# A two-layer hybrid trunk on one core: products put in order of length, the first output projection in wider blocks, and background steps called more often

## The chip, the core and the metric

The kernel runs on one core of a Trainium2 chip. The metric is the device time of one execution in microseconds (us); the profile is of one execution, taken apart from the timed runs. TensorE (PE) multiplies, VectorE (DVE) and ScalarE (ACT) do elementwise work, GpSimd (POOL) small work and some transfers, and SyncE (SP) issues the weight transfers. A difference of under 0.2% is about what a measurement of this kernel can't tell from none.

## The reference, cut to what matters

256 tokens of 2048 features pass through two layers. Layer 0 is a gated delta net, layer 1 an attention over chunks; each has one input projection of 2048 to 8192 features (q, k, v and the gate z), a mixer over 16 heads of 128, and an output projection of 2048 to 2048, whose result is added to the input.

```
def gated_deltanet(h, w_in, conv_w, a_log, dt_bias, out_norm_w, w_out):
    proj = h @ w_in
    qkv = silu(causal_depthwise_conv(proj[..., :3 * A_INNER], conv_w))
    z = proj[..., 3 * A_INNER:4 * A_INNER]
    ...                      # q, k normed; beta, g per head from 32 more columns
    decay = exp(where(tri_incl, gc[..., :, None] - gc[..., None, :], -inf))
    sol = triangular_solve(eye + lower, rhs)          # per chunk of 64
    ...                      # scan over the chunks gives o
    o = rms_norm(o, out_norm_w) * silu(z)
    return o.reshape(bsz, t, A_INNER) @ w_out

def chunk_band_attention(h, w_in, q_norm_w, k_norm_w, rel_bias, w_out):
    ...                      # softmax over a band of keys, times silu(z)
    return o @ w_out

for i in range(DEPTH):
    h = h + mixer[i](rms_norm(h, norm_w[i]))
```

## The kernel before

All matrices are f32. A product of f32 matrices is made of three products of rounded parts: the weights are split into `whi` and `wlo`, the activations into a high and a low part (`xb[:, kt, 0]` and `xb[:, kt, 1]`), and high x high, high x low and low x high are summed in PSUM. The features of a 2048-wide operand lie in 16 slices of 128, which the text calls kt 0 to 15.

**The weights** come in 320 chunks of 512 KB, in the order of the list `plan`. `chunk` uses one and first calls `fetch` until the chunk three further on is asked for: a transfer into `wt` (SP), a cast to `whi` on ACT (L191) and a subtraction to `wlo` on DVE (L192). There are three buffers of `whi` and of `wlo`, so a chunk's cast waits until TensorE has finished with the chunk three before it.

**The kinds of block.** `half` makes 256 output features: a chunk is four kt of 256 columns, and for each kt and each of two slices of 128 features (s) there are two products with the weights as the stationary operand, one of 512 moving columns (`whi` on both parts of the activations, L232) and one of 256 (`wlo` on the high part, L233). The text calls these two a pair; a half block is 32 pairs. `features` makes 512 output features out of three products of 256 columns for each kt and s (L224, L226, L227), a triple; a block is 64 triples in eight chunks of two kt. `tokens` makes 512 features with the activations as the stationary operand, in products of 512 columns (L239 to L241). A block accumulates in a tile `psp` of PSUM, of which there are two; `joined` moves a half block out (ACT copies the second product's part into `ev`, DVE adds the rest, L288 and L289), and `ev` has two buffers too. Small products, such as the transposes, use `pss`.

**The background.** Everything that isn't a projection is written as generators in two lanes, `bgq` and `bg2`. After each kt (each second kt in a half block) `chunk` calls `step(rate)`, which advances `rate` times one generator to its next `yield`, the lanes in turn; `drain` runs all of them to their end. So the place of a small product in TensorE's order, and of a vector operation in DVE's, follows from these calls, and from a scheduler in the framework which sorts the instructions of each engine by a timeline of its own.

**Order of the work.** Layer 0: q (a block in 512 features, then six half blocks), k (eight half blocks), three token blocks of z, v (eight half blocks), the last token block of z, then the first output projection. `decays` makes the decay factors, `q_conv` and `k_small` convolve, `inversion` solves the triangular systems, `v_small`, `v_back` and `gated` make a group of four heads of the mixer's output and split it into `gmem` (tile `g`); group gi gives kt 4gi to 4gi+3 of the output projection, and `ready` holds a product back until its kt is done.

**The first output projection before** (kernel end of `tile_hybrid_trunk`): eight half blocks. The first two are cut: kt 0 to 11 of both, then `drain`, then kt 12 to 15 of both, since the last head group comes last. `ha_small` takes a finished block, adds x (fetched by POOL's queue into tile `dl`, which the mixer has used until then) and splits the sum for layer 1.

Of the kernel before, what the change touches and what calls it, by code (L numbers as in the profile page):

```python
# [7 lines left out]
F32 = mybir.dt.float32  # L8
# [3 lines left out]
ALU = mybir.AluOpType  # L12
AX = mybir.AxisListType

P = 128
D = 2048
T = 256
H = 16
KT = D // P
# [4 lines left out]
NWARM = 12  # L24
TIE0 = 4
TIE = 2


C_CONV = 0
# [10 lines left out]
def tile_hybrid_trunk(  # L40
# [11 lines left out]
    nc = tc.nc  # L52
# [24 lines left out]
    xv = xT.rearrange("(k p) t -> p k t", p=P)  # L77
# [51 lines left out]
    def wide(w, col, c0=0, c1=CPB):  # L129
        return [(w, col, c, 512) for c in range(c0, c1)]  # L130
# [4 lines left out]
    def halves(w, col, n):  # L135
        return [x for j in range(n) for x in half(w, col + 256 * j)]
# [9 lines left out]
    def cut_halves(w, col):  # L146

        p = []
        for c0, c1 in ((0, CUTH), (CUTH, CPH)):
            for j in range(2):  # L150
                p += half(w, col + 256 * j, c0, c1)
        return p + halves(w, col + 512, 6)

    plan += cut_halves(a_w_out, 0)
    plan += cut_halves(b_w_in, 6144)
    for gi in range(4):
        plan += wide(b_w_in, 4096 + 512 * gi)
# [48 lines left out]
    def step(n=1):  # L206

        while now:
            now.pop(0)()
        for _ in range(n):  # L210
            lanes = (bgq, bg2) if turn[0] else (bg2, bgq)
            turn[0] ^= 1
            for lane in lanes:
                if advance(lane):
                    break
# [10 lines left out]
        pe.matmul(ps, lhsT=hi[:, j, fs], rhs=xb[:, kt, 1, :], start=False, stop=False, skip_group_check=True)  # L226
        pe.matmul(ps, lhsT=lo[:, j, fs], rhs=xb[:, kt, 0, :], start=False, stop=(kt == KT - 1), skip_group_check=True)  # L227

    def features2(ps, s, j, kt, hi, lo, xb):

        fs = slice(s * P, (s + 1) * P)
        pe.matmul(ps, lhsT=hi[:, j, fs], rhs=xb[:, kt, :, :], start=(kt == 0), stop=False, skip_group_check=True)  # L232
        pe.matmul(ps[:, 0, :], lhsT=lo[:, j, fs], rhs=xb[:, kt, 0, :], start=False, stop=(kt == KT - 1),  # L233
                  skip_group_check=True)

    def tokens(ps, t, j, kt, hi, lo, xb):
        ts_ = slice(t * P, (t + 1) * P)
# [2 lines left out]
        pe.matmul(ps, lhsT=xh, rhs=lo[:, j, :], start=False, stop=False)  # L240
        pe.matmul(ps, lhsT=xl, rhs=hi[:, j, :], start=False, stop=(kt == KT - 1))  # L241

    KINDS = {"features": (features, 4), "half": (features2, 2), "tokens": (tokens, 2)}

    def chunk(kind, ps, xb, rate=1, pre=None):
        i = state["use"]
        state["use"] += 1
        while state["next"] < min(i + 1 + LOOK, len(plan)):
            fetch()
        hi, lo = fetched.pop(i)  # L250
        kc = KC * 512 // plan[i][3]
        ks = [plan[i][2] * kc + j for j in range(kc)]
        f, ns = KINDS[kind]
        if i == len(plan) - 1:

            out_pre(ps)
            for s in range(ns):
                fs = slice(s * P, (s + 1) * P)
                for j, kt in enumerate(ks):
                    for w, a in ((hi, 0), (hi, 1), (lo, 0)):  # L260
                        pe.matmul(ps[:, s, 0, :], lhsT=w[:, j, fs], rhs=xb[:, kt, a, :], start=False,
                                  stop=(kt == KT - 1 and w is lo), skip_group_check=True)
                out_part(s, ps)
            return
        for j, kt in enumerate(ks):
            if pre is not None:
                pre(kt)
            for s in range(ns):
                f(ps[:, s], s, j, kt, hi, lo, xb)
            if kind != "half" or j % 2:  # L270
                step(rate)

    def acc(kind):

        shape = {"features": [P, 4, T], "half": [P, 2, 2, T], "tokens": [P, 2, 512]}[kind]
        return psp.tile(shape, F32, name="psp", tag="psp")

    def block(kind, xb, rate=1, pre=None):
        ps = acc(kind)
        for _ in range(CPH if kind == "half" else CPB):  # L280
            chunk(kind, ps, xb, rate, pre)
        return ps
# [423 lines left out]
    def ready(mem):  # L706

        def pre(kt):
            while mem["done"] <= kt:
                step()  # L710
        return pre
# [97 lines left out]
        split(x_sb[:, kt, :], kt, 0, xb)  # L809

    for gi in range(4):
        ps = pair(xb) if gi else block("features", xb, pre=x_split)
        if gi == 0:
            bgq.append(x_stats())
        bgq.append(q_conv(gi, ps))
        if gi == 0:
            bgq.append(decays())
        else:
            if gi == 1:
                bgq.append(q_rest(0))  # L820
            bgq.append(q_rest(gi))
    for gi in range(4):
        bgq.append(k_small(gi, pair(xb)))
    for gi in range(3):
        ps = block("tokens", xb)
        if gi == 0:
            drain()
        bgq.append(za_small(gi, ps))
        if gi == 0:
            bgq.append(inversion())  # L830
# [7 lines left out]

    hmem = {}

    def ha_small(n, ps):
        if n == 0:
            m = slot("dl", 48)
            hmem["m"] = m
            hmem["h"] = m[:, :2 * D].rearrange("p (k t) -> p k t", k=KT)
            hmem["x"] = split_tiles()
            hmem["s"] = m[:, 8192:9216].rearrange("p (j t) -> p j t", j=4)
            hmem["done"] = 0
        xb, h = hmem["x"], hmem["h"][:, 2 * n:2 * n + 2, :]
        j = n // 2  # L850
        if n % 2 == 0:
            ks = slice(4 * j, 4 * j + 4)
            nc.gpsimd.dma_start(out=hmem["h"][:, ks, :], in_=xv[:, ks, :])
        ev = work.tile([P, 2, T], F32, name="ev", tag="ev")
        act.copy(out=ev, in_=ps[:, :, 1, :])  # L855
        yield 1
        if n in (0, 2):

            dve.tensor_copy(out=hmem["h"][0:1, 4 * j + 8, 0:1], in_=ev[0:1, 0, 0:1])
        dve.tensor_tensor(out=h, in0=ps[:, :, 0, :], in1=h, op=ALU.add)  # L860
        dve.tensor_tensor(out=h, in0=h, in1=ev, op=ALU.add)
        yield 1
        for i in range(2):
            split(h[:, i, :], 2 * n + i, 1, xb)
            hmem["done"] = 2 * n + i + 1
            yield 1
        if n % 2:
            squares4(hmem["h"][:, 4 * j:4 * j + 4, :], hmem["s"][:, j, :])
            yield 1

# [14 lines left out]
                    z=slot("tt", 16).rearrange("p (h t) -> p h t", h=H))  # L885
        yield 1

    def a_done(j, ps):
        bgq.append(ha_small(j, ps))

    pa = [acc("half") for _ in range(2)]
    for n in (CUTH, CPH - CUTH):
        for j in range(2):
            if n != CUTH and j == 0:
                drain()
            for _ in range(n):
                chunk("half", pa[j], gmem["b"], 3, ready(gmem))
            if n != CUTH:
                a_done(j, pa[j])
    for j in range(2, 8):  # L900
        a_done(j, block("half", gmem["b"], 2))


    bgq.append(b_setup())
# [231 lines left out]
```

## Time and profile before

| | |
|---|---|
| three timed runs | 1033.37, 1034.61, 1035.04 us (median 1034.61) |
| profiled execution: its time, its span | 1032.16 us, 1030.5 us |
| TensorE busy | 1009.8 us (98% of the span) |
| VectorE busy | 698.7 us (68%) |
| ScalarE busy | 525.4 us (51%) |
| granted TensorE clock, mean | 0.993 of full |

The profiled execution is 1.7 us longer than its span (launch and end), and 2.45 us shorter than the median of the runs. Ends of matmuls are modelled and overlap, so "busy" on TensorE is no measure of speed; the spacing of starts is.

### The profile page before, as it was taken

What the parts mean: (1) busy time and instruction counts of PE and PEld (TensorE: products, weight loads), DVE (VectorE), ACT (ScalarE), POOL (GpSimd) and SP (SyncE); (2) the same over time, 40 slices, a digit from 0 to 9 for tenths busy, and PEclk for the clock granted to TensorE, in tenths of its full rate; (3) what the DMA queues carried; (4) which work ended last, traced back from release to release, by engine and by line L of the source; (5) the groups of instructions that cost most, each with busy time, mean ns of one, the idle gap of its engine ahead of it and who ended that gap; (6) DMA issues with size and microseconds to landing.
All of it is one profiled execution on the core that took longest, in us unless ns stands there. A gap on an engine that the chain in (4) does not pass through costs nothing.

```text
span 1030.5 us, 15332 instructions
## 1 busy us (share of the span) xinstructions
PE 1009.8 (98%) x5966; PEld 874.0 (85%) x5966; DVE 698.7 (68%) x1117; ACT 525.4 (51%) x726; POOL 74.4 (7%) x91
## 2 busy tenths in 40 slices
PE   8999999999999999987999999999999999999998
PEld 7988888887888989886888888888888888889986
DVE  7789899997997688655666555444456666666553
ACT  8465765455445555443554444444445545555442
POOL 1004000212000000001000000000011010101000
PEclk9999999999999999998999999999999999999999
DMA  9654565554773454543656776666665555554562
GB/s 309 177 164 132 157 182 164 147 162 141 209 197 107 123 160 132 161 162 123 207 188 181 221 217 213 188 200 188 198 186 169 158 166 161 163 162 147 177 221 72
DMA packets 137832, 177.54 MB, mean 172 GB/s; under 512 B 7584, under 2 KB 97824, under 8 KB 137760
## 3 DMA queue, kind: packets, MB, share of 16 engines
q1 hardware_dynamic: 136608, 172.38, 56.3%
q0 software_dynamic: 1152, 4.19, 1.1%
q8 instruction: 46, 0.75, 0.3%
q14 instruction: 26, 0.21, 0.1%
HBM read 174.46 MB, written 2.10 MB: 171 GB/s over the span
## 4 chain that ended last, share of the span: by engine, by line
PE 93%; DVE 3%; ACT 1%; issue 1%; DMA 0%; SPq 0%; POOL 0%; DVEq 0%; ACTq 0%; POOLq 0%
PE psp L232 29%; PE psp L233 15%; PE psp L240 11%; PE psp L239 11%; PE psp L241 11%; PE psp L227 2%; PE psp L226 2%; PE psp L224 2%; PE pss L540 2%; DVE wlo L192 1%; PE pss L737 1%; PE pss L972 1%; PE pss L991 1%; PE pss L1027 1%; ACT whi L191 1%
## 5 line engine op out<-in xcount | busy, mean ns | idle before, releaser
L192 DVE TENSOR_TENSOR wlo<-wt,whi 128x1024 fp32r<-128x1024 f32 (+1 forms) x321 | 392.8, 1226 | 254.1 <-ACT whi L191 250.7
L191 ACT CAST whi<-wt 128x1024 fp32r<-128x1024 f32 (+1 forms) x321 | 336.3, 1049 | 403.8 <-PE psp L232 187.8
L232 PE MATMUL psp<-xb,whi 128*128 128x512 f32 x960 | 341.0, 398 | 2.1 <-DVE ev L289 2.0
L233 PE MATMUL psp<-xb,wlo 128*128 128x256 f32 x960 | 270.3, 282 | 0.0
L232 PEld LDWEIGHTS psp<-xb,whi 128*128 128x128 f32 x960 | 180.8, 189 | 43.8 <-DVE ev L289 2.7
L241 PE MATMUL psp<-whi,xb 128*128 128x512 f32 x512 | 201.2, 393 | 0.0
L240 PE MATMUL psp<-wlo,xb 128*128 128x512 f32 x512 | 200.9, 392 | 0.3 <-DVE wlo L192 0.3
L239 PE MATMUL psp<-whi,xb 128*128 128x512 f32 x512 | 199.8, 390 | 0.0
L233 PEld LDWEIGHTS psp<-xb,wlo 128*128 128x128 f32 x960 | 181.9, 189 | 1.5 <-DVE wlo L192 0.5
L232 PE MATMUL psp<-g,whi 128*128 128x512 f32 x376 | 135.9, 405 | 2.6 <-ACT ev L855 1.6
L240 PEld LDWEIGHTS psp<-wlo,xb 128*128 128x128 f32 x512 | 96.1, 188 | 20.7 <-DVE wlo L192 1.2
L239 PEld LDWEIGHTS psp<-whi,xb 128*128 128x128 f32 x512 | 96.2, 188 | 19.7
L241 PEld LDWEIGHTS psp<-whi,xb 128*128 128x128 f32 x512 | 96.2, 188 | 19.4
L233 PE MATMUL psp<-g,wlo 128*128 128x256 f32 x376 | 106.5, 284 | 0.0
L232 PEld LDWEIGHTS psp<-g,whi 128*128 128x128 f32 x376 | 71.8, 191 | 20.8 <-ACT ev L855 1.9
L233 PEld LDWEIGHTS psp<-g,wlo 128*128 128x128 f32 x376 | 72.3, 192 | 0.2
L483 DVE SCALAR_TENSOR_TENSOR cv<-raw,sm,cv 128x255 f32<-128x255 f32 (+2 forms) x144 | 62.0, 479 | 1.7 <-ACT cv L481 1.5
L224 PE MATMUL psp<-g,whi 128*128 128x256 f32 x128 | 36.8, 288 | 0.0
L226 PE MATMUL psp<-g,whi 128*128 128x256 f32 x128 | 36.7, 287 | 0.0
L227 PE MATMUL psp<-g,wlo 128*128 128x256 f32 x128 | 36.3, 284 | 0.0
L955 POOL TENSOR_SCALAR ssn<-ssn,uh 128x4 f32<-128x4 f32 x16 | 8.3, 530 | 271.9 <-DVE ssn L953 271.9
L481 ACT ACTIVATE cv<-raw,sm 128x256 f32<-128x256 f32 x48 | 21.4, 500 | 7.7 <-DVE raw L304 4.8
(240 smaller groups left out, 988.2 us busy)
## 6 DMA issues: line engine op xcount, KB each, us to landing
wt<-in_b_w_in_dram SPq DMA_DIRECT2D x128, 512.0 KB, 3.7
wt<-in_a_w_in_dram SPq DMA_DIRECT2D x127, 512.0 KB, 4.0
wt<-in_a_w_out_dram SPq DMA_DIRECT2D x32, 512.0 KB, 3.4
wt<-in_b_w_out_dram SPq DMA_DIRECT2D x32, 512.0 KB, 3.8
g<-in_xT_dram SPq DMA_DIRECT2D x8, 256.0 KB, 4.5
dl<-in_xT_dram POOLq DMA_DIRECT2D x4, 512.0 KB, 5.5
dl<-in_relb_dram POOLq DMA_DIRECT2D x4, 512.0 KB, 5.1
out_dram<-cv SPq DMA_DIRECT2D x2, 512.0 KB, 3.6
```

The lines of the kernel that those rows point to most:

```text
L191: act.copy(out=hi[:, js], in_=wt[:, js])
L192: dve.tensor_tensor(out=lo[:, js], in0=wt[:, js], in1=hi[:, js].bitcast(F32), op=ALU.subtract)
L224: pe.matmul(ps, lhsT=hi[:, j, fs], rhs=xb[:, kt, 0, :], start=(kt == 0 and s % 2 == 0), stop=False, skip_group_check=True)
L226: pe.matmul(ps, lhsT=hi[:, j, fs], rhs=xb[:, kt, 1, :], start=False, stop=False, skip_group_check=True)
L227: pe.matmul(ps, lhsT=lo[:, j, fs], rhs=xb[:, kt, 0, :], start=False, stop=(kt == KT - 1), skip_group_check=True)
L232: pe.matmul(ps, lhsT=hi[:, j, fs], rhs=xb[:, kt, :, :], start=(kt == 0), stop=False, skip_group_check=True)
L233: pe.matmul(ps[:, 0, :], lhsT=lo[:, j, fs], rhs=xb[:, kt, 0, :], start=False, stop=(kt == KT - 1), skip_group_check=True)
L239: pe.matmul(ps, lhsT=xh, rhs=hi[:, j, :], start=(kt == 0), stop=False)
L240: pe.matmul(ps, lhsT=xh, rhs=lo[:, j, :], start=False, stop=False)
L241: pe.matmul(ps, lhsT=xl, rhs=hi[:, j, :], start=False, stop=(kt == KT - 1))
L481: act.activation(out=cv[:, i, :], in_=raw[:, i, :], func=AF.Copy, scale=conv_w(i0 + i, 3))
L483: dve.scalar_tensor_tensor(out=cv[:, i, s:], in0=raw[:, i, :T - s], scalar=conv_w(i0 + i, 3 - s), in1=cv[:, i, s:], op0=ALU.mult, op1=ALU.add)
```

## The change

Three edits. In half blocks the products of two kt (GROUP) are issued by length: the four of 512 columns, then the four of 256. The first two blocks of the first output projection (eight half blocks before) become blocks of 512 features of the kind `features`, cut at the same kt 12; four half blocks follow. And `decays` goes into the second lane, the pairs of q call `step(2)`, the second and third token block of z too; the cut blocks call `step(2)` after each kt, where they called `step(3)` after each second one.

```
@@ -151,7 +152,10 @@
-    plan += cut_halves(a_w_out, 0)
+    for c0, c1 in ((0, CUT), (CUT, CPB)):
+        for j in range(2):
+            plan += wide(a_w_out, 512 * j, c0, c1)
+    plan += halves(a_w_out, 1024, 4)
@@ -226,12 +230,16 @@
-    def features2(ps, s, j, kt, hi, lo, xb):
-        fs = slice(s * P, (s + 1) * P)
-        pe.matmul(ps, lhsT=hi[:, j, fs], rhs=xb[:, kt, :, :], start=(kt == 0), stop=False, skip_group_check=True)
-        pe.matmul(ps[:, 0, :], lhsT=lo[:, j, fs], rhs=xb[:, kt, 0, :], start=False, stop=(kt == KT - 1),
-                  skip_group_check=True)
+    def features2(ps, hi, lo, js, ks, xb):
+        both = [(s, j) for j in js for s in range(2)]
+        for s, j in both:
+            pe.matmul(ps[:, s], lhsT=hi[:, j, s * P:(s + 1) * P], rhs=xb[:, ks[j], :, :], start=(ks[j] == 0), stop=False,
+                      skip_group_check=True)
+        for s, j in both:
+            pe.matmul(ps[:, s, 0, :], lhsT=lo[:, j, s * P:(s + 1) * P], rhs=xb[:, ks[j], 0, :], start=False,
+                      stop=(ks[j] == KT - 1), skip_group_check=True)
@@ -262,13 +270,21 @@
+        if kind == "half":
+            for j in range(0, kc, GROUP):
+                js = range(j, j + GROUP)
+                if pre is not None:
+                    for jj in js:
+                        pre(ks[jj])
+                features2(ps, hi, lo, js, ks, xb)
+                step(rate)
+            return
@@ -809,12 +825,12 @@
-        ps = pair(xb) if gi else block("features", xb, pre=x_split)
+        ps = pair(xb, 2) if gi else block("features", xb, pre=x_split)
...
-            bgq.append(decays())
+            bg2.append(decays())
...
-        ps = block("tokens", xb)
+        ps = block("tokens", xb, 2 if gi else 1)
@@ -846,25 +863,28 @@
+        two = len(ps.shape) == 4
+        if two:
+            ev = work.tile([P, 2, T], F32, name="ev", tag="ev")
+            act.copy(out=ev, in_=ps[:, :, 1, :])
...
+        dve.tensor_tensor(out=h, in0=ps[:, :, 0, :] if two else ps, in1=h, op=ALU.add)
+        if two:
+            dve.tensor_tensor(out=h, in0=h, in1=ev, op=ALU.add)
@@ -885,20 +905,20 @@
-    pa = [acc("half") for _ in range(2)]
-    for n in (CUTH, CPH - CUTH):
+    pa = [acc("features") for _ in range(2)]
+    for n in (CUT, CPB - CUT):
         for j in range(2):
-            if n != CUTH and j == 0:
+            if n != CUT and j == 0:
                 drain()
             for _ in range(n):
-                chunk("half", pa[j], gmem["b"], 3, ready(gmem))
-            if n != CUTH:
-                a_done(j, pa[j])
-    for j in range(2, 8):
-        a_done(j, block("half", gmem["b"], 2))
+                chunk("features", pa[j], gmem["b"], 2, ready(gmem))
+            if n != CUT:
+                a_done(j, pa[j], 4 * j, 4 * j + 4)
+    for j in range(4):
+        a_done(j + 2, block("half", gmem["b"], 2), 8 + 2 * j, 10 + 2 * j)
```

The order of the built programs shows where this moves instructions. First TensorE at the cut of the first output projection, before: L760 to L762 are the last products of the mixer (`v_back`, last group), L798 the transposes of `gated` for that group, L232 and L233 the output projection.

```order
L760 MATMUL pss<-dl 128x128
L761 MATMUL pss<-dl 128x128
L762 MATMUL pss<-dl 128x128
L798 MATMUL pss<-ident,dl 128x128 x8
L232 MATMUL psp<-g,whi 128x512
L233 MATMUL psp<-g,wlo 128x256
L232 MATMUL psp<-g,whi 128x512
```

The same place after (the lines of the mixer are 16 higher, the products of the output projection are L228, L230 and L231). Between the two pieces stand 76 products of the output projection, counted without the rows shown of the second piece's transposes; 175 stand ahead of the first piece.

```order
L776 MATMUL pss<-dl 128x128
L777 MATMUL pss<-dl 128x128
L778 MATMUL pss<-dl 128x128
L230 MATMUL psp<-g,whi 128x256
L231 MATMUL psp<-g,wlo 128x256
...
L230 MATMUL psp<-g,whi 128x256
L814 MATMUL pss<-ident,dl 128x128 x2
L231 MATMUL psp<-g,wlo 128x256
L228 MATMUL psp<-g,whi 128x256
L230 MATMUL psp<-g,whi 128x256
L231 MATMUL psp<-g,wlo 128x256
L814 MATMUL pss<-ident,dl 128x128 x6
```

Where nothing stood between the mixer's last product and the transposes, 76 products stand there now; after the transposes 33 more come before the first one that needs kt 12 (288 products of the two cut blocks don't need it: 12 kt, 4 slices, 3 products, 2 blocks).

Second, ScalarE early in the k stage, before: L509 are squares of `q_rest`, L191 the weight cast, L288 the copy that moves a half block out of `psp`, L481 the first taps of a convolution.

```order
L191 CAST whi<-wt 128x1024 x2
L509 ACTIVATE raw<-pss 128x512 x2
L191 CAST whi<-wt 128x1024
L288 COPY ev<-psp 128x512
L481 ACTIVATE cv<-raw,sm 128x256 x4
L191 CAST whi<-wt 128x1024
L288 COPY ev<-psp 128x512
```

And after (L525, L195, L304 and L497 are the same lines there):

```order
L195 CAST whi<-wt 128x1024
L525 ACTIVATE raw<-pss 128x512 x2
L195 CAST whi<-wt 128x1024 x2
L497 ACTIVATE cv<-raw,sm 128x256 x2
L304 COPY ev<-psp 128x512
L497 ACTIVATE cv<-raw,sm 128x256 x2
L195 CAST whi<-wt 128x1024
L304 COPY ev<-psp 128x512
```

The copy out of `psp` has moved behind two taps of the convolution, and a weight cast ahead of it; the rest of the stage's order is nearly as it was.

Third, TensorE in any half block, before:

```order
L232 MATMUL psp<-xb,whi 128x512
L233 MATMUL psp<-xb,wlo 128x256
L232 MATMUL psp<-xb,whi 128x512
L233 MATMUL psp<-xb,wlo 128x256
```

and after:

```order
L238 MATMUL psp<-xb,whi 128x512 x4
L241 MATMUL psp<-xb,wlo 128x256 x4
```

The same products stand in runs of four of one length.

## Rows read from the trace of the kernel before

**Rows 1.** The page: busy us (share of the span) xinstructions of each engine, and the chain that ended last, by engine.

```profile
PE 1009.8 (98%) x5966; PEld 874.0 (85%) x5966; DVE 698.7 (68%) x1117; ACT 525.4 (51%) x726; POOL 74.4 (7%) x91
...
PE 93%; DVE 3%; ACT 1%; issue 1%; DMA 0%; SPq 0%; POOL 0%; DVEq 0%; ACTq 0%; POOLq 0%
```

**Rows 2.** Busy time of the stretch around the cut of the first output projection: us from and to, their length, then busy us of PE, PEld, DVE, ACT and POOL with the number of instructions, the granted TensorE clock (1.00 is full), the DMA share and GB/s.

```profile
461.00:481.00 20.00, 11.47 (x46) 9.28 (x46) 8.32 (x13) 4.89 (x7) 4.17 (x4) 0.74 0.26 85
```

**Rows 3.** TensorE in order of time at the cut of the first output projection: start us, us, then the instruction; in brackets the idle time before it and who ended it.

```profile
460.64 0.39 PE L762 MATMUL pss<-dl 128*128 128x128 f32 x2
466.99 2.15 PE L798 MATMUL pss<-ident,dl 128*128 128x128 f32 x8 [5.97 <-DVE dl L694]
470.06 0.80 PE L232 MATMUL psp<-g,whi 128*128 128x512 f32 x1 [0.92 <-DVE g L803]
...
470.86 0.63 PE L232 MATMUL psp<-g,whi 128*128 128x512 f32 x1
...
475.35 0.54 PE L232 MATMUL psp<-g,whi 128*128 128x512 f32 x1
...
478.16 0.28 PE L233 MATMUL psp<-g,wlo 128*128 128x256 f32 x1
480.07 0.47 PE L232 MATMUL psp<-g,whi 128*128 128x512 f32 x1 [1.64 <-ACT ev L855]
```

**Rows 4.** The chain of work that ended last, in the same stretch: start us, us, what.

```profile
461.06 0.61 ACT dl L763
461.69 1.23 DVE so L769
463.25 1.65 POOL ro L772
464.92 1.30 DVE dl L778 x2
...
469.26 0.76 DVE g L803
```

**Rows 5.** TensorE in order of time, first output projection, later on; 54 rows between the first and the last, L232 and L233 in turn.

```profile
499.93 0.40 PE L232 MATMUL psp<-g,whi 128*128 128x512 f32 x1
...
509.47 0.40 PE L232 MATMUL psp<-g,whi 128*128 128x512 f32 x1
```

**Rows 6.** The same in the z blocks of the second layer; 55 rows between, in turn.

```profile
599.75 0.27 PE L233 MATMUL psp<-xb,wlo 128*128 128x256 f32 x1
...
609.46 0.27 PE L233 MATMUL psp<-xb,wlo 128*128 128x256 f32 x1
```

**Rows 7.** The same in the k blocks of the first layer; 33 rows between, in turn.

```profile
129.94 0.28 PE L233 MATMUL psp<-xb,wlo 128*128 128x256 f32 x1
...
135.95 0.28 PE L233 MATMUL psp<-xb,wlo 128*128 128x256 f32 x1
```

**Rows 8.** The same in the second output projection, a block in 512 features; 59 rows between, L224, L226 and L227 in turn.

```profile
965.75 0.28 PE L227 MATMUL psp<-g,wlo 128*128 128x256 f32 x1
...
972.95 0.28 PE L227 MATMUL psp<-g,wlo 128*128 128x256 f32 x1
```

**Rows 9.** The same in the v blocks of the second layer (kind `tokens`); 44 rows between, L239, L240 and L241 in turn.

```profile
649.71 0.39 PE L241 MATMUL psp<-whi,xb 128*128 128x512 f32 x1
...
659.91 0.39 PE L241 MATMUL psp<-whi,xb 128*128 128x512 f32 x1
```

**Rows 10.** TensorE in order of time between two k blocks; L540 is the k products of one head, three of 512 columns and three of 256, and stands among the products of a half block.

```profile
192.02 0.85 PE L540 MATMUL pss<-kT 128*128 128x512 f32 x3
192.71 0.40 PE L232 MATMUL psp<-xb,whi 128*128 128x512 f32 x1
...
193.99 0.52 PE L540 MATMUL pss<-kT 128*128 128x256 f32 x3
194.35 0.28 PE L233 MATMUL psp<-xb,wlo 128*128 128x256 f32 x1
```

**Rows 11.** A wait in the k stage: TensorE, then VectorE, then ScalarE, in order of time.

```profile
115.15 0.50 PE L232 MATMUL psp<-xb,whi 128*128 128x512 f32 x1 [1.98 <-DVE ev L289]
...
114.41 0.68 DVE L289 TENSOR_TENSOR ev<-psp,ev 128x512 f32<-128x512 f32 x1
...
112.79 0.59 ACT L288 COPY ev<-psp 128x512 f32<-128x512 f32 x1 [1.47 <-DVE raw L304]
113.27 1.70 ACT L481 ACTIVATE cv<-raw,sm 128x256 f32<-128x256 f32 x4
```

**Rows 12.** Busy time of a stretch of the first layer's k stage; columns as in Rows 2.

```profile
150.00:200.00 50.00, 50.00 (x288) 43.61 (x287) 47.48 (x101) 27.43 (x35) 3.31 (x3) 1.00 0.55 151
```

**Rows 13.** Groups by line and shape: VectorE, then ScalarE (after the bar: busy us, mean ns of one; then idle time before).

```profile
L192 DVE TENSOR_TENSOR wlo<-wt,whi 128x1024 fp32r<-128x1024 f32 x319 | 391.5, 1229 | 252.8 <-ACT whi L191 249.5 <-PE psp L233 2.4
L483 DVE SCALAR_TENSOR_TENSOR cv<-raw,sm,cv 128x254 f32<-128x254 f32 x48 | 21.7, 477 | 0.0
L304 DVE TENSOR_TENSOR raw<-ev,rB 128x512 f32<-128x512 f32 x22 | 14.8, 686 | 0.2
L1071 DVE TENSOR_TENSOR cv<-psp,dl 128x1024 f32<-128x1024 f32 x2 | 2.5, 1225 | 1.4 <-PE psp L227 1.4
L191 ACT CAST whi<-wt 128x1024 fp32r<-128x1024 f32 x319 | 335.0, 1052 | 402.7 <-PE psp L232 187.8 <-PE psp L241 147.3 <-PE psp L226 20.5
```

**Rows 14.** The page: DMA issues, out<-in engine op xcount, KB each, median us from issue to landing.

```profile
dl<-in_xT_dram POOLq DMA_DIRECT2D x4, 512.0 KB, 5.5
```

More of the change, by code (lines that the diff above doesn't have):

```diff
@@ L26 @@
 TIE = 2
+GROUP = 2
 C_CONV = 0
@@ L241, in tokens @@
         pe.matmul(ps, lhsT=xl, rhs=hi[:, j, :], start=False, stop=(kt == KT - 1))
-    KINDS = {"features": (features, 4), "half": (features2, 2), "tokens": (tokens, 2)}
+    KINDS = {"features": (features, 4), "half": (None, 2), "tokens": (tokens, 2)}
     def chunk(kind, ps, xb, rate=1, pre=None):
@@ L269, in chunk @@
                 f(ps[:, s], s, j, kt, hi, lo, xb)
-            if kind != "half" or j % 2:
-                step(rate)
+            step(rate)
     def acc(kind):
@@ L839, in tile_hybrid_trunk, with ha_small @@
     hmem = {}
-    def ha_small(n, ps):
+    def ha_small(n, ps, ks):
         if n == 0:
@@ L848, in ha_small @@
             hmem["done"] = 0
[L849 to L855, printed above, removed]
-        yield 1
[L857 to L861, printed above, removed]
+        xb, h, k0 = hmem["x"], hmem["h"][:, ks, :], ks.start
+        if k0 % 4 == 0:
+            qs = slice(k0, k0 + 4)
+            nc.gpsimd.dma_start(out=hmem["h"][:, qs, :], in_=xv[:, qs, :])
+        two = len(ps.shape) == 4
+        if two:
+            ev = work.tile([P, 2, T], F32, name="ev", tag="ev")
+            act.copy(out=ev, in_=ps[:, :, 1, :])
+        yield 1
+        if n < 2:
+            dve.tensor_copy(out=hmem["h"][0:1, k0 + 8, 0:1], in_=ps[0:1, 0, 0:1])
+        dve.tensor_tensor(out=h, in0=ps[:, :, 0, :] if two else ps, in1=h, op=ALU.add)
+        if two:
+            dve.tensor_tensor(out=h, in0=h, in1=ev, op=ALU.add)
         yield 1
-        for i in range(2):
-            split(h[:, i, :], 2 * n + i, 1, xb)
-            hmem["done"] = 2 * n + i + 1
+        for k in range(ks.start, ks.stop):
+            split(hmem["h"][:, k, :], k, 1, xb)
+            hmem["done"] = k + 1
             yield 1
-        if n % 2:
+        if ks.stop % 4 == 0:
+            j = ks.stop // 4 - 1
             squares4(hmem["h"][:, 4 * j:4 * j + 4, :], hmem["s"][:, j, :])
@@ L886, in b_setup, with a_done @@
         yield 1
-    def a_done(j, ps):
-        bgq.append(ha_small(j, ps))
-    pa = [acc("half") for _ in range(2)]
-    for n in (CUTH, CPH - CUTH):
+    def a_done(n, ps, k0, k1):
+        bgq.append(ha_small(n, ps, slice(k0, k1)))
+    pa = [acc("features") for _ in range(2)]
+    for n in (CUT, CPB - CUT):
         for j in range(2):
-            if n != CUTH and j == 0:
+            if n != CUT and j == 0:
                 drain()
             for _ in range(n):
-                chunk("half", pa[j], gmem["b"], 3, ready(gmem))
-            if n != CUTH:
-                a_done(j, pa[j])
-    for j in range(2, 8):
-        a_done(j, block("half", gmem["b"], 2))
+                chunk("features", pa[j], gmem["b"], 2, ready(gmem))
[3 more added lines that the diff above has]
+        a_done(j + 2, block("half", gmem["b"], 2), 8 + 2 * j, 10 + 2 * j)
     bgq.append(b_setup())
```

## The prediction, as it was put on record before the run

> **What bounds the kernel now.** Read first the page. TensorE is busy for 98% of the span and the chain that ended last runs over it for 93%, DVE for 3% [rows 1]. So time can be won only where TensorE waits, or where its products come closer together. The waits by place come next. One stretch stands out: around 461 to 481 us TensorE is busy for 11.5 of 20 us and its granted clock is 0.74, a mixture of the 2.4 and the 1.2 GHz level [rows 2]. This is the cut of the first output projection. In order of time the reader sees TensorE end the mixer's last products at 460.64, wait 6 us, do eight transposes, resume at 470.06 with products 640 ns per pair apart, and wait once more until 480.07 [rows 3]. The chain there says for what: square, row sum, GpSimd's power, two scalings, the transposes, the split into `g` [rows 4]. All of this is the last head group on its way to kt 12 to 15; no other product is left to issue, because the two cut half blocks are used up. Elsewhere TensorE waits little (the largest other wait seen is 2 us, at 115 [rows 11]), and its pace is the spacing of its products.
>
> **Spacings.** A pair takes 27 steps of 353.3 ns in the first output projection ((509.47 - 499.93) / 27 [rows 5]), 346.8 ns in layer 1's z ((609.46 - 599.75) / 28 [rows 6]) and 353.5 ns in k ((135.95 - 129.94) / 17 [rows 7]). Three products of 256 columns, a triple, take 360 ns: 60 steps of 120 [rows 8]. Products of 512 columns in a row take 226.7 ns each (10.20 / 45 [rows 9]).
>
> **The stall at the cut (term A).** From 460.64 to 480.07 are 19.4 us. The work in it is 16 pairs (5.6 us at 353), eight transposes and the last two small products (10 of about 0.11 us, 1.1 us), 6.7 us together. Lost: 12.7 us, made up of 6.1 us before the transposes, 2.2 us around them (466.99 to 470.06, less 0.9), 2.5 us in the eight pairs at the lower clock (470.06 to 475.35, less 2.8 [rows 3]) and 1.8 us until `psp` is free (478.16 to 480.07, less 0.12).
> After the change 288 products (12 kt, 4 slices, 3 products, 2 blocks) need no kt of the last group, and take 288 x 0.12 = 34.6 us where the cut half blocks gave 48 pairs, 17 us. By the order the mixer's last product stands behind 175 of them, and 76 stand between it and the transposes: 9.1 us for a chain which took 6.3 (460.7 to 466.99 [rows 3]). DVE now has weight splits between the links of the chain. The split of chunk 138 stands ahead of the scalings; its cast waits until TensorE has finished with chunk 135, that is product 192, 17 products or 2 us behind the mixer's last, and ends with its split at about 2 + 1.05 + 1.23 = 4.3 us [rows 13], when the power ends too (4.2 us behind [rows 4]). Two scalings of two operations each follow (464.92 to 466.99 [rows 4] for the first three). So the transposes can start at some 6.5 of 9.1 us. Then 33 products (4 us) and the transposes (0.9) cover the split into `g`, 3 us before (466.99 to 470.02 [rows 4]). Next late would be `psp`: the first block's buffer is wanted again after the second block's last 48 products, 5.8 us, and is emptied by one operation of 128x1024 (1.23 us [rows 13], the same form) which needs x from POOL's queue. POOL issues that once `dl` is free, at the transposes; 5.5 us to land [rows 14], about 1.8 for two issues, against (33 + 48) x 0.12 = 9.7 us. All three are covered by 2 us or more, so I take the whole stall as removed, and the clock as staying at 2.4 GHz since TensorE doesn't idle: **-12.7 us**. Each us by which a cover fails comes back one to one; at most all 12.7.
>
> **Triples for pairs (term B).** 128 pairs become 128 triples: 128 x (360 - 353.3) = **+0.9 us**; with the z pair's 346.8 it would be 1.7. Four copies to `ev` and four additions go, on engines with idle time: nothing.
>
> **Order by length (term C).** 1208 pairs are left in half blocks (38 x 32, less the eight of the last chunk, which is written apart). In fours they are made of 3 steps from 512 to 512, one from 512 to 256, three from 256 to 256 and one back. Before, such steps are seen where k's products stand: three of 512 take 192.02 to 192.71, 230 ns each, three of 256 take 193.99 to 194.35, 120 each [rows 10]; token blocks say 226.7 for the first [rows 9]. The change of length costs 350 ns there and back, the pair itself. So a pair becomes (3 x 226.7 to 230, 3 x 120, and 347 to 353) / 4 = 347 to 351 ns against 346.8 to 353.5 now. I take 2.5 ns less, between the ends: 1208 x 2.5 = **-3.0 us**; the bounds are -7.9 (353.5 to 347) and +5.1 (346.8 to 351).
> The Trainium skill ("TensorE: Matmul & The Clock Gate", Back-to-back issue gap) gives a spacing of N / 2.4 + 2.5 ns, which hangs on a product's own length alone: 325 ns for a pair in any order. By it this edit is worth nothing; the rows differ from it by 22 to 29 ns, so something it leaves out is there, but equal lengths in a row (120 and 226.7, where it says 109 and 216) show that too.
>
> **More steps, second lane (term D).** The scheduler leaves q and k nearly as they were. What moves is seen early in k: there TensorE waited 2 us because ACT's copy out of `psp` (L288) came late and DVE's addition behind it [rows 11]. In the new order a weight cast and two taps of the convolution stand ahead of that copy. The taps are 1.70 us for four [rows 11], so two delay it by about 0.9: **+1.0 us**, between -2 (the wait vanishes, as more steps might bring) and +3. The doubled rate in the token blocks hastens `inversion`, whose end feeds only a mixer that has a longer cover now: nothing.
>
> **Sum.** -12.7 + 0.9 - 3.0 + 1.0 = -13.8 us, against the profiled execution's 1032.2 us (span 1030.5 and 1.7 around it): 1018.4. The median of the runs stands 2.4 us higher, so the time expected there is **1020.8 us**, faster by 1.3%. Within 0.2%, 2.1 us, a measurement can't tell the kernels apart.
>
> **Rivals.**
> *The order of length does nothing* (C is 0): spacings follow the products' own lengths. For it, layer 1's z runs at 346.8 already in turns; against it, the 353 elsewhere. 1023.8 us. The page named above says the same.
> *The order gives much more*: turns of length are what makes 353 out of the 320 ns that 768 columns take at 2.4 GHz (half of the 640 at the lower clock [rows 3]). All of it back would be 1208 x 31 = 37 us, 987 us; a third, 12 us, 1012. Against it, uniform runs of 120 and 226.7 sum to 347.
> *The cover at the cut is too short*: DVE's splits delay the chain by 4 us more than reckoned, or x lands late. 4 to 8 us come back, and more with the clock: 1025 to 1029.
> *Slower*: the steps crowd DVE. In k it is busy 47.5 of 50 us [rows 12]. A convolution is 12 x 0.48 + 2 x 0.69 = 7.1 us of DVE [rows 13]; at four steps per chunk it falls into 1.25 chunks (3.5 us of TensorE) with 1.5 us of splits, 5.1 us too late. Three buffers forgive two chunks less cast and split, 5.6 - 2.3 = 3.3, so TensorE waits 1.8 us. In all 11 half-block convolutions that is 20 us, 1041; it takes nine of them to reach the time before. For it, DVE's load; against it, the built order, in which the convolutions keep their places.
>
> **Chances.** Forecast (1015 to 1023) 0.48; no gain from the order (1023 to 1025) 0.2; much more from it (below 1015) 0.12; short cover (1025 to 1031) 0.12; slower 0.05, and 0.03 for a mixture that ends where it began. Faster by over 0.2%: 0.92, the same 0.03, slower 0.05. The likeliest case's own range is 1015 to 1024; the range for 8 in 10 takes in the short cover and part of the larger gain, 1012 to 1029.
>
> **What would show it.** A: no wait over 1 us and a clock of 1.00 between the mixer's last products and layer 1; L814 without idle time before it; a first output projection shorter by some 12 us. B: 120 ns steps there. C: steps of 227 to 230 and 120 in half blocks, pairs of 347 to 351. D: a wait of about 3 us at the same place in k. Wrong would be: a wait of TensorE for `wlo` or `ev` in q, k or v that wasn't there, or a pair outside 340 to 355.

## The result, and the profile after

The changed kernel takes 1023.70 us (median of 4 runs, 1023.05 to 1024.37) beside 1033.99 us for the kernel before (4 runs, 1032.30 to 1035.04): ratio 0.9905, 95% interval 0.9889 to 0.9922. The forecast was 1020.8, its range 1012 to 1029. So it is faster, as forecast, by 10.3 us where 13.8 had been reckoned. The profiled execution has a span of 1022.4 us, 8.1 less than before's.

The page after answers to [rows 1]. Its lines are the engines' busy time and the chain that ended last.

```profile
PE 1007.9 (99%) x6094; PEld 881.1 (86%) x6094; DVE 694.8 (68%) x1111; ACT 520.2 (51%) x720; POOL 76.3 (7%) x91
...
PE 95%; DVE 2%; ACT 1%; DMA 1%; issue 1%; SPq 0%; DVEq 0%; ACTq 0%
```

The next rows give busy time by stretch; the columns are those of [rows 2]. The first row is the cut of the output projection, which stood at 11.47 us busy and a clock of 0.74.

```profile
461.00:481.00 20.00, 20.00 (x172) 20.00 (x171) 11.23 (x16) 8.50 (x11) 2.20 (x2) 1.00 0.44 137
112.00:122.00 10.00, 7.98 (x36) 6.65 (x35) 10.00 (x17) 4.78 (x9) 0.00 (x0) 0.83 0.57 161
118.00:122.00 4.00, 3.96 (x12) 3.33 (x13) 4.00 (x9) 0.49 (x2) 0.00 (x0) 0.57 0.45 129
10.00:20.00 10.00, 8.27 (x54) 7.87 (x53) 8.53 (x14) 8.62 (x17) 2.96 (x4) 0.83 0.99 345
```

TensorE is full there now, at 1.00. The other three rows are places where time was lost instead: in the first trace of the kernel before, the granted clock was 1.00 in each of them.

TensorE in order of time answers to [rows 3]: the mixer's last products, products of the cover, the transposes (L814), which no wait precedes.

```profile
468.94 0.39 PE L778 MATMUL pss<-dl 128*128 128x128 f32 x2
...
478.28 0.38 PE L814 MATMUL pss<-ident,dl 128*128 128x128 f32 x2
478.42 0.36 PE L231 MATMUL psp<-g,wlo 128*128 128x256 f32 x1
...
478.98 0.82 PE L814 MATMUL pss<-ident,dl 128*128 128x128 f32 x6
```

And VectorE in the same stretch, which answers to [rows 4]:

```profile
470.00 1.22 DVE L785 TENSOR_REDUCE so<-dl 128x8 f32<-128x1024 f32 x1 [1.07 <-ACT dl L779]
...
472.36 1.23 DVE L196 TENSOR_TENSOR wlo<-wt,whi 128x1024 fp32r<-128x1024 f32 x1 [0.94 <-ACT whi L195]
473.50 1.28 DVE L794 TENSOR_TENSOR dl<-pss,ro 128x512 f32<-128x512 f32 x2
474.82 1.30 DVE L710 TENSOR_TENSOR dl<-dl,kT 128x512 f32<-128x512 f32 x2
```

The chain ends at 476.12, 7.2 us behind the mixer's last product, and the transposes come at 478.28: the cover holds with 2.2 us to spare, though a weight split stands inside the chain.

The whole stage is bounded by its own first product and the first of layer 1's z. Before:

```profile
436.84 0.39 PE L232 MATMUL psp<-g,whi 128*128 128x512 f32 x1
...
547.98 0.40 PE L232 MATMUL psp<-xb,whi 128*128 128x512 f32 x1
```

After:

```profile
441.10 0.28 PE L228 MATMUL psp<-g,whi 128*128 128x256 f32 x1
...
540.01 1.09 PE L238 MATMUL psp<-xb,whi 128*128 128x512 f32 x4
```

That is 111.1 us before and 98.9 after: 12.2 us won in the stage. But the stage begins 4.3 us later than before. What TensorE waited for in the program after says where (us in total, times, longest):

```profile
PE psp L238 <- DVE ev L305: 2.0, 1, 2.0
PE psp L248 <- DVE wlo L196: 1.6, 1, 1.6
PE psp L238 <- DVE raw L323: 1.6, 1, 1.6
PE psp L228 <- ACT whi L195: 1.3, 2, 1.0
```

The first is the wait in k of [rows 11], no longer than it was, but now with the lower clock behind it (0.57 from 118 to 122 us). The second (264 us, gates) and the third (50 us, behind the decays' transposes) are new. The fourth is at the start: weights landed late at 10 us in this execution.

The pairs, ordered by length, in the output projection (answers to [rows 5]; 11 rows of four products each between) and in z (answers to [rows 6]; 13 between). The text says "in fours" for this order and "in turns" for the old one, where a product of 512 columns and one of 256 alternate:

```profile
500.72 1.09 PE L238 MATMUL psp<-g,whi 128*128 128x512 f32 x4
...
509.14 1.09 PE L238 MATMUL psp<-g,whi 128*128 128x512 f32 x4
```

```profile
599.84 1.09 PE L238 MATMUL psp<-xb,whi 128*128 128x512 f32 x4
...
609.66 1.09 PE L238 MATMUL psp<-xb,whi 128*128 128x512 f32 x4
```

(509.14 - 500.72) / 24 = 350.8 ns and (609.66 - 599.84) / 28 = 350.7 ns a pair: one value in both stages, between the 353.3 and the 346.8 of before.

### The profile page after: what moved, and what is told of

The parts are those of the page before. It is cut to its first block, busy times and chain, and to the rows that moved or that the text cites. A ratio compares the mean times of both kernels' runs of the same rounds, so it can differ in the third digit from the quotient of the medians.

```text
span 1022.4 us, 15569 instructions
## 1 busy us (share of the span) xinstructions
PE 1007.9 (99%) x6094; PEld 881.1 (86%) x6094; DVE 694.8 (68%) x1111; ACT 520.2 (51%) x720; POOL 76.3 (7%) x91
## 4 chain that ended last, share of the span: by engine, by line
PE 95%; DVE 2%; ACT 1%; DMA 1%; issue 1%; SPq 0%; DVEq 0%; ACTq 0%
PE psp L238 27%; PE psp L241 14%; PE psp L248 11%; PE psp L249 11%; PE psp L247 11%; PE psp L231 4%; PE psp L228 4%; PE psp L230 4%; PE pss L556 2%; PE pss L753 1%; PE pss L992 1%; PE pss L1011 1%; PE pss L1047 1%; DMA wt<-in_a_w_in_dram 1%; DVE wlo L196 1%; PE pss L1037 1%
## 5 line engine op out<-in xcount | busy, mean ns | idle before, releaser
L195 ACT CAST whi<-wt 128x1024 fp32r<-128x1024 f32 (+1 forms) x321 | 336.7, 1050 | 410.9 <-PE psp L238 164.0
L238 PE MATMUL psp<-xb,whi 128*128 128x512 f32 x960 | 265.7, 396 | 3.6 <-DVE ev L305 2.0
L238 PEld LDWEIGHTS psp<-xb,whi 128*128 128x128 f32 x960 | 165.0, 190 | 25.9 <-DVE ev L305 2.2
L241 PEld LDWEIGHTS psp<-xb,wlo 128*128 128x128 f32 x960 | 148.4, 189 | 20.1
L241 PE MATMUL psp<-xb,wlo 128*128 128x256 f32 x960 | 157.6, 283 | 0.0
L228 PE MATMUL psp<-g,whi 128*128 128x256 f32 x256 | 73.4, 287 | 0.0
L230 PE MATMUL psp<-g,whi 128*128 128x256 f32 x256 | 73.3, 287 | 0.0
L231 PE MATMUL psp<-g,wlo 128*128 128x256 f32 x256 | 72.7, 284 | 0.0
L238 PE MATMUL psp<-g,whi 128*128 128x512 f32 x248 | 67.7, 394 | 0.0
L499 DVE SCALAR_TENSOR_TENSOR cv<-raw,sm,cv 128x254 f32<-128x254 f32 (+2 forms) x144 | 61.8, 474 | 0.1
L230 PEld LDWEIGHTS psp<-g,whi 128*128 128x128 f32 x256 | 49.1, 192 | 0.2
L228 PEld LDWEIGHTS psp<-g,whi 128*128 128x128 f32 x256 | 49.1, 192 | 0.1
L231 PEld LDWEIGHTS psp<-g,wlo 128*128 128x128 f32 x256 | 49.1, 192 | 0.1
L238 PEld LDWEIGHTS psp<-g,whi 128*128 128x128 f32 x248 | 42.4, 189 | 5.7
L241 PEld LDWEIGHTS psp<-g,wlo 128*128 128x128 f32 x248 | 38.1, 189 | 5.3
```

The source lines that it names most:

```text
L195: act.copy(out=hi[:, js], in_=wt[:, js])
L228: pe.matmul(ps, lhsT=hi[:, j, fs], rhs=xb[:, kt, 0, :], start=(kt == 0 and s % 2 == 0), stop=False, skip_group_check=True)
L238: pe.matmul(ps[:, s], lhsT=hi[:, j, s * P:(s + 1) * P], rhs=xb[:, ks[j], :, :], start=(ks[j] == 0), stop=False, skip_group_check=True)
L241: pe.matmul(ps[:, s, 0, :], lhsT=lo[:, j, s * P:(s + 1) * P], rhs=xb[:, ks[j], 0, :], start=False, stop=(ks[j] == KT - 1), skip_group_chec ...
L499: dve.scalar_tensor_tensor(out=cv[:, i, s:], in0=raw[:, i, :T - s], scalar=conv_w(i0 + i, 3 - s), in1=cv[:, i, s:], op0=ALU.mult, op1=ALU.add)
```

## The experiments

The theory after this reading: A and B hold as reckoned, C is small, D is larger than reckoned. The rivals: the order of the products made the gain, or it made the new waits too. The first four runs do one part of the change alone, or leave one out.

**e1, the output projection alone.** The kernel before with the diff's plan, `ha_small`, `a_done` and the loops below it; pairs in turns.

> Only the first output projection is changed (two feature blocks ahead of four half blocks, their background of two steps per call); pairs stay in turns, decays and steps per call as before. My theory (terms A and B of the prediction, read again in the trace after): -11.8 to -12.3 us, so about 1022 beside 1034, no idle time at the cut, output projection 99 us long instead of 111. Rival (the gain of after came from the order of the products): -3 us or less, about 1031.

Measured: 1022.34 us, ratio 0.9904 (0.9875 to 0.9933), so -9.9 us by the runs; the span is 1017.7, 12.8 less than that of before. There is no wait at the cut; its row answers to the first one of after:

```profile
461.00:481.00 20.00, 20.00 (x169) 20.00 (x169) 11.63 (x13) 8.18 (x9) 3.93 (x3) 1.00 0.68 211
```

This part alone makes the whole gain; the rival falls. About 1.7 of the 12.8 us by the spans are not the cut's: the first trace of before has a granted clock of 0.83 from 322 to 332 us, that of e1 has 1.00 there.

**e2, the order alone.** The kernel before with the new `features2` and the loop over `GROUP`.

> Only the order by length within two weight slices is changed. Predicted: -3.0 us (1031). Read again from the trace after (a pair 350.9 ns everywhere, against 353.3 in q, k and the first output projection and 346.8 in layer 1's z): -1 to -2 us, about 1032.5. Rival (length alone sets the spacing): 0. Rival (the order frees the weight loads): -10 or more. The stall of 6 us at the cut of the output projection is expected to stand in all three.

Measured: 1031.08 us, ratio 0.9987 (0.9970 to 1.0004), -1.3 us, not told apart from nothing. The wait at the cut stands (6.0 us). The wait of 1.6 us for `wlo` in the gates is there too, so it belongs to the order, not to the steps.

**e3, decays and steps alone.**

```
-        ps = pair(xb) if gi else block("features", xb, pre=x_split)
+        ps = pair(xb, 2) if gi else block("features", xb, pre=x_split)
-            bgq.append(decays())
+            bg2.append(decays())
-        ps = block("tokens", xb)
+        ps = block("tokens", xb, 2 if gi else 1)
```

> Only the decays' lane and the steps per call in q and in two of the three gate blocks are changed. Predicted: +1.0 us. Read again from the trace after: +2 to +4 us (1036 to 1038), with a new wait of TensorE near 50 us behind the decays' transposes and a longer one near 263 us in the gates. Rival: 0 (those waits of after come from the order of the products, which shifts the schedule), about 1034.

Measured: 1036.71 us, ratio 1.0033 (1.0012 to 1.0054), +3.4 us. Its waits of TensorE in q and k:

```profile
PE psp L232 <- DVE ev L289: 2.6, 1, 2.6
PE psp L232 <- DVE raw L307: 1.1, 1, 1.1
```

The wait at 50 us is there with the products in turns, so the rival that the order made it falls. The lower clock behind the wait in k (0.57 from 118 to 122) is there too; e5 will show that it needs no change of the kernel. I had expected a longer wait in the gates as well, and was wrong: none over 0.2 us stands there.

**e4, the change without the steps.** `GROUP` and the output projection; e3's three lines as before.

> The whole change without the decays' lane and the steps per call, so the output projection and the order by length together. If the steps cost 2 to 4 us, as read in the trace after: 1020 to 1021.5, faster than the whole change by as much, without the wait near 50 us. If they cost nothing: 1023.7 as the whole change. If they pay for themselves: over 1024.

Measured: 1020.56 us, ratio 0.9887 (0.9863 to 0.9912). The span is 1017.4; the wait at 50 us is gone, that in k is 1.4 us, one of 1.4 us stands at 95 us before L471 (0.7 us in before), and the clock stays at 1.00.

**The spacing of pairs.** The traces of e1 and e3 held a surprise. Pairs in turns took 353 ns in z in both; in e3's output projection they took 347. These are e3's rows in the output projection (57 between) and in z (55 between):

```profile
499.87 0.39 PE L232 MATMUL psp<-g,whi 128*128 128x512 f32 x1
...
509.92 0.39 PE L232 MATMUL psp<-g,whi 128*128 128x512 f32 x1
```

```profile
599.78 0.40 PE L232 MATMUL psp<-xb,whi 128*128 128x512 f32 x1
...
609.68 0.40 PE L232 MATMUL psp<-xb,whi 128*128 128x512 f32 x1
```

10.05 / 29 = 346.6 ns and 9.90 / 28 = 353.6 ns: [rows 5] and [rows 6] exchanged, with the same products. **e5, the kernel before once more,** asks whether this hangs on the code at all.

> The kernel before, unchanged, traced a second time. If the spacing of products in turns (353.3 ns a pair in the output projection, 346.8 in layer 1's z) belongs to a stage, as the prediction took it, both values come again at the same places. If it is one of two modes that a stretch falls into, as the trace with the steps alone suggests (346.7 in the output projection and 353.3 in z, the same lines and the same plan), at least one of the two stages may show the other value.

```profile
499.72 0.39 PE L232 MATMUL psp<-g,whi 128*128 128x512 f32 x1
...
509.77 0.40 PE L232 MATMUL psp<-g,whi 128*128 128x512 f32 x1
```

The same program now gives 346.6 ns (10.05 / 29) in the output projection, where its first trace gave 353.3. In z it gives 346.6 again. So a stretch in turns runs in one of two modes, and at this place the mode changes from one execution to the next. It does not do so everywhere: in all five traces in turns (both of before, e1, e3, e9) the pairs take 353 ns in the second output projection (975 to 1025 us) and 347 in the last k blocks (from 200 us).

The output projection is 2.3 us shorter here than in the first trace, 108.9 us:

```profile
442.16 0.39 PE L232 MATMUL psp<-g,whi 128*128 128x512 f32 x1
...
551.03 0.39 PE L232 MATMUL psp<-xb,whi 128*128 128x512 f32 x1
```

Yet this execution took 1035.11 us. A wait without a visible cause before L650 took 2.9 us, where the first trace has 0.7, and the clock was lower: 0.66 from 322 to 332 us (0.83 in the first trace), and in k, where the first trace has 1.00:

```profile
112.00:122.00 10.00, 8.02 (x38) 6.68 (x37) 9.97 (x18) 4.66 (x8) 0.00 (x0) 0.83 0.65 196
```

```profile
115.52 0.50 PE L232 MATMUL psp<-xb,whi 128*128 128x512 f32 x1 [1.98 <-DVE ev L289]
```

So the unchanged kernel too can have the lower clock behind the wait in k, with the same wait of 2.0 us.

**e6, the whole change once more,** beside its parts on one chip.

> The whole change, unchanged, timed beside its own parts. If the decays' lane and the steps cost what e3 and e4 say, 2 to 3.5 us more than the change without them (1020.6), so 1022.5 to 1024.5; the pair spacing 350.9 ns in every stage again. The lower clock from 11 to 16 us in the first trace of after is expected here only if it belongs to the code; if it is chance, the trace may be without it and its span 2.5 us shorter.

Measured: 1022.38 us, ratio 0.9892 (0.9867 to 0.9916). The ordered pairs take 350.8 ns again; the waits at 50 us (1.6) and in k (2.0) are there again, so these belong to the code. The lower clock from 118 us is there again too, but e5 has it without the change. The lower clock from 11 to 16 us is not there: 1.00. In its place this trace has 0.57 from 50 to 54 us, behind the wait of 1.6 us, where the first trace of after has 1.00.

**e7, with the decays' lane; e8, with the steps per call.** Both have the output projection and the order; e7 adds `bg2.append(decays())`, e8 the two other lines of e3's diff.

> Output projection, order by length and the decays in the second lane, with the steps per call of q and gates as before. If the lane is what costs: 1022.5 to 1024 and a wait of TensorE of 1.5 to 2 us behind the decays' transposes near 50 us. If the steps per call are what costs: 1020.5, no such wait.

> Output projection, order by length and two steps per call in q and in two gate blocks, with the decays in the first lane as before. If the steps per call cost: 1022 to 1024, with a longer wait at the first k block near 115 us and the lower clock behind it. If the lane costs: 1020.5.

Measured: e7 1032.96 us, ratio 0.9993 (0.9977 to 1.0010), far outside what I had expected; e8 1020.10 us, ratio 0.9872 (0.9845 to 0.9900). In e7 TensorE stands at the first k block:

```profile
112.86 0.60 PE L523 MATMUL pss<-ident,g 128*128 128x128 f32 x4
121.82 1.65 PE L238 MATMUL psp<-xb,whi 128*128 128x512 f32 x3 [8.36 <-DVE ev L305]
```

```profile
118.49 1.21 DVE L527 TENSOR_REDUCE ssq<-raw 128x8 f32<-128x1024 f32 x1
119.73 1.29 DVE L320 TENSOR_TENSOR raw<-ev,rB 128x512 f32<-128x512 f32 x2
121.07 0.69 DVE L305 TENSOR_TENSOR ev<-psp,ev 128x512 f32<-128x512 f32 x1
```

The second fence is VectorE just ahead: from 116.2 us on it is busy without a gap. ScalarE's copy out of the accumulator waits for L320, which reads the old `ev`, and L320 stands behind work of q (L527 among it, which ran at 110.8 us in before). In e8 this wait is gone altogether (the chain of waits shows none on `ev`), in the whole change it is 2.0 us. So the lane delays q's work into k and the steps pull it back: lane without steps +11 us (e7 to e4, by the ratios). Of these the trace shows 7.0 us of wait (8.4 less e4's 1.4) and, by estimate, 2.6 of lower clock (0.50 from 117 to 127 us, with TensorE busy for 5.2 of them). Lane with steps costs +2.3 us (e6 to e8, by the medians; the intervals of their ratios overlap), steps without the lane nothing that can be measured. By the ratios lane and steps together cost 0.5 us (e6 to e4), which the intervals can't tell from nothing.

**e9, a shorter cut.** e1 with one constant more:

```
+    CUTA = CUTH
-    for c0, c1 in ((0, CUT), (CUT, CPB)):
+    for c0, c1 in ((0, CUTA), (CUTA, CPB)):
-    for n in (CUT, CPB - CUT):
+    for n in (CUTA, CPB - CUTA):
-                chunk("features", pa[j], gmem["b"], 2, ready(gmem))
+                chunk("features", pa[j], gmem["b"], 3, ready(gmem))
```

> The kernel of e1 (feature blocks in the first output projection, nothing else), but cut after 3 of 8 weight slices instead of 6: 144 products of 120 ns ahead of the cut, 17.3 us, as much time as the 48 pairs of before (48 times 353 ns, 17.0 us), and three steps per call so that as many steps lie in it (36). If the length of the cover removed the stall: idle time of 5 to 7 us at the cut again, the clock low behind it, and 8 to 11 us lost to e1 (1030 to 1033). If the kind of the products or the shorter tail of the mixer removed it: no stall, about 1022.

Measured: 1025.11 us, ratio 0.9917 (0.9893 to 0.9941). My expectation fell: no wait at the cut.

```profile
464.36 0.39 PE L766 MATMUL pss<-dl 128*128 128x128 f32 x2
464.50 0.36 PE L231 MATMUL psp<-g,wlo 128*128 128x256 f32 x1
...
474.42 1.03 PE L802 MATMUL pss<-ident,dl 128*128 128x128 f32 x8
```

82 products still stand between the mixer's last and the transposes, and 216 in the cover in all, as many as in e1 itself (218; 251 in the whole change), where the cut written in the code leaves 144. The scheduler had moved products from behind the cut ahead of the transposes: slices 4 to 6 need no head of the last group. So this run does not take the cover away, and does not tell its length from its kind. What it shows is that the written cut does not set the cover; the products that need no kt of the last group and find an accumulator open do (12 kt in two blocks, 288 products of 120 ns, or 48 pairs).

**e10 and e11, what sets an ordered pair.** Both start from e8. e10 walks the feature halves outside (`for s in range(2) for j in js`); e11 has `GROUP = 4` and `step(rate * GROUP // 2)`.

> The kernel of e8, but the four long products (and the four short ones) go through the weight slices of one feature half before the other, so that two in a row add into the same half of the accumulator, not in alternation. Long products behind one another take 226.7 ns in the token blocks and 233.6 in the ordered half blocks. If the alternation of accumulators costs the 7 ns: 228 to 230 ns, a pair of 346 or less, and 5 to 7 us faster than e8 (1013 to 1015). If not: 233 to 235 ns and 1020 as e8.

> The kernel of e8 with groups of four weight slices instead of two: eight long products, then eight short ones, and as many steps in half as many calls. If the spacing is set by the neighbours alone as in after (233.6 long to long, 228.3 long to short, 118.6 and 118.1): (7 x 233.6 + 228.3 + 7 x 118.6 + 118.1) / 8 = 351.5 ns a pair, +0.7 us from the spacing, 1020 to 1022. If a longer run of equal products is cheaper, as the prediction had it: below 347 ns and 5 us faster.

Measured: e10 1020.13 us, ratio 0.9872 (0.9837 to 0.9907), 233.7 ns from 512 to 512 in z (233.6 in the whole change): the alternation of accumulators is not what costs. e11 1018.75 us, ratio 0.9861 (0.9824 to 0.9898). Its z rows, eight long, eight short:

```profile
601.86 2.00 PE L238 MATMUL psp<-xb,whi 128*128 128x512 f32 x8
603.70 1.12 PE L241 MATMUL psp<-xb,wlo 128*128 128x256 f32 x8
...
607.45 2.00 PE L238 MATMUL psp<-xb,whi 128*128 128x512 f32 x8
```

5.59 / 16 = 349.4 ns a pair, 2 less than reckoned from the neighbours alone and 1.4 less than in fours: the first four long products of a run take about 232 ns each, the last four 228, and from the sixth to the eighth it is 226.4 to 226.9, as in the token blocks. A longer run is a little cheaper; 1208 pairs make 1.7 us of that, and the medians differ by 1.4, which the scatter of the runs would hide (e8 1018.83 to 1022.38, e11 1017.41 to 1020.72).

**e12, one step per call in all gate blocks,** else e11.

> The kernel of e11 with one step per call in all gate blocks, as before the change, so that of the steps only two per call in q is left. If the pace of the gates feeds the wait of 2.1 us on the low weights near 256 us, that wait is shorter and the time 1016.5 to 1018; if that wait comes from the order alone (it stands in e2 and e4 too, which have one step per call), it stays and the time is 1018 to 1019.5. Slower than 1020.5 if the gates' second step had taken work out of the v blocks.

Measured: 1017.95 us, ratio 0.9843 (0.9825 to 0.9860): the fastest, 5 us below the whole change by e6's ratio, and the intervals of the two don't meet. The wait for `wlo` stands (1.6 us at 257; in e11 it was 1.6 too, not the 2.1 of my expectation), so it comes from the order, which puts a weight split behind a transpose on VectorE (L616 in the trace after, 2.1 us, itself 3.1 us behind ScalarE).

## Why the prediction was right, and where it wasn't

**A, right in place and size.** Reckoned -12.7 with B's +0.9, so -11.8; the stage is 12.2 us shorter than in the first trace of before and 10.0 shorter than in e5, whose pairs ran in the other mode. e1 measures -9.9 (-12.9 to -6.9) by the runs, -12.8 by the spans. Of the chain: 6.5 us reckoned, 7.2 found, with the weight split in it; spare 2.2 us, as the "2 us or more" had it. The clock is 1.00 in the stretch and no wait for `psp` came. That the edit removed the stall is shown by e1; that the cover's length did it, and not the kind of its products, is argued from the rows (76 products where none stood), for e9, meant to show it by a run, kept e1's cover.

**B, right for one mode.** The products of the triples take 120 ns each in the new blocks; they bring no wait. The +0.9 us holds against pairs of 353 ns; against those of e5 it is the 1.7 that the prediction names beside it.

**C, the step that failed is its basis.** The working took 353.3 and 346.8 ns as what the output projection and z cost in turns, and the ordered pair as cheaper than the mean of the two. In turns both values occur in either stage, from one execution to another (e3, e5); in fours it is 350.8 in both. Averaged over all pairs of a trace that follow one another without a break at full clock (1000 or more), it is 350.8 ns in the first trace of before and 349.4 to 351.7 in the five traces in turns, and 350.6 to 350.9 in fours: on average the order changes nothing. The order wins 2.5 ns a pair against the one mode and loses 4 against the other. The steps from 512 to 512 were taken at 226.7 to 230 ns, from token blocks and k's products; they are 233.6.

Reckoned -3.0; measured -1.3 (-3.1 to +0.4), and e4 less e1 -1.8 us, with intervals that overlap. Both contain a new wait of 1.6 us for `wlo`, which nothing in the prediction had. The rival "the order does nothing" is not excluded; "much more" is.

By the formula of the Trainium skill ("TensorE: Matmul & The Clock Gate", Back-to-back issue gap) a pair takes, by estimate, 325 ns in any order; the section gives it for an isolated product and says that in a stream of weight loads and products both set the spacing. The runs show 346.6, 353.6, 350.8 and 349.4 for the same two products, so the formula does not give the spacing here, and its 216 ns for 512 columns is 233.6 in fours.

**D, misplaced.** Reckoned +1.0 at one place, the wait in k growing to 3 us. It did not grow (2.0). The clock fell behind it (4 us at 0.57, 1.7 us lost), but so it did in e5, without the change. What is new is a wait of 1.6 us at 50 us: L323, which empties the accumulator of q's first block, now stands behind the decays' transposes and their copy. Measured: +3.4 us alone (1.2 to 5.6); beside the other two edits 0.5 (e6 to e4), which can't be told from nothing. The prediction reckoned the lane and the steps as one term; they are opposed. The lane costs, the steps mend most of it.

**The rest.** The reckoned 13.8 us less the measured 10.3 leaves 3.5 us: by the runs 1.9 from A and B (e1) and 1.7 from C (e2), each with its reckoned value inside the interval. D, +0.5 or +3.4 by the pair of runs that one takes, has no size that could be set against the reckoned +1.0. The measured 1023.70 lies just outside the forecast's own band (1015 to 1023) and in that of the rival without a gain from the order, whose 1023.8 it meets. That C came out near nothing speaks for this rival; that the time fits to 0.1 us is chance, for by the runs A and B are short of its sum too. A wait for a weight split did appear, as the prediction's sign of being wrong had it ("a wait for `wlo` or `ev` in q, k or v that wasn't there"), but in the gates, and from the order instead of the steps.

## What to carry to other kernels

Where TensorE stalls behind a long chain of small operations, look for products that depend on nothing in the chain: open accumulators with as much independent work as the chain is long, and read off the rows between its ends how much is to spare. Time the parts of a bundle of edits apart: here one part made the whole gain, and without the decays' lane (and with longer runs of one length and one step per call in the gates) the kernel is 5 us faster. A spacing read from one stretch of one execution is not the price of an instruction; before costing a change of 1% by it, see it in a second trace.

## What the runs showed of the hardware

- Products of 512 and 256 columns in turn have two spacings, 346.6 and 353.5 ns a pair, in the same code at the same place in different executions; ordered by length there is one (350.8 in fours, 349.4 in eights). What chooses the mode stays open.
- The runs of the kernels in turns scatter by 5.7 to 8.9 us (before beside e1 to e4 1028.95 to 1037.58, e3 1032.37 to 1040.55), those of the ordered ones by 1.3 to 3.9 (e2 1029.28 to 1033.20). The mean granted clock goes with the time: of those 23 executions of before the three at 0.990 have spans of 1034.4 to 1035.6 us, the four at 0.995 1027.0 to 1028.3. By estimate 0.005 of the clock is 5 us (0.005 x 1030, TensorE being busy nearly throughout), so by this the clock makes the larger part. The means of the pairs in turns, 349.4 to 351.7 ns, make 2.8 us over 1208 pairs; that they are the rest is not shown.
- Whether the clock falls behind a wait of 2 us is not fixed by its length: eight traces have the wait in k at 1.96 to 2.02 us, and the clock fell behind it in five of them (0.83 from 112 to 122 us: both of after, e5, e9, e12), not in the first of before, in e1 and in e11. One kernel, before, did both. Behind the waits of 1.6 us it fell once in two traces at 50 us (e6, not after) and once in nine in the gates (e2).
- 512 to 512 takes 226.7 ns in token blocks and 233.6 in half blocks in fours. The alternation of accumulators is not the reason (e10). In eights the sixth to eighth step take 226.4 to 226.9 (e11), so it is the first steps of a run that are dearer; why stays open.
